# Decoder block on one core: order of split casts, small products and last outputs

## The chip, the core and the metric

The kernel runs on one core of a Trainium2 chip: TensorE (PE, with its weight loads PEld), VectorE (DVE), ScalarE (ACT), GpSimd (POOL) and SyncE (SP), each with its own instruction stream, and 16 DMA engines. The metric is device time in microseconds (us). The kernel before took 1091.79 us, the median of three runs (1090.93 to 1091.82).

## The reference

The input is x of 1024 rows by 1024 columns, all in float32. After a mixer (pooling and windowed attention, gated) comes the MLP, in which the change lies:

```python
x = x + _rmsnorm(mix, g_mix_post[l])
h2 = _rmsnorm(x, g_mlp_pre[l])
ff = jnp.einsum('bsf,fd->bsd',
                jnp.square(jax.nn.relu(jnp.einsum('bsd,df->bsf', h2, w_up[l]))), w_down[l])
x = x + _rmsnorm(ff, g_mlp_post[l])
```

w_up has 1024 by 4096 elements, w_down 4096 by 1024.

## The kernel before, in words

**Precision.** A float32 operand is split into a high part in the matmul's reduced format and a low rest: `split` (L99 to L104) is a cast on ACT (L101) and a subtraction on DVE (L104). Each product of two operands is three matmuls (`PASSES`): high x high, high x low and low x high.

**Fewer products.** Both MLP matmuls are done as a two by two block scheme with seven products instead of eight, so that sums and differences of blocks are operands too.

*Up projection* (class `Pairs`, L510 on). The 32 column blocks of w_up are taken in 16 pairs. Each pair p has seven products of 12 matmuls (4 blocks of the inner size, three passes), 128x512 each: `m1` to `m7`. `m6`, `m7` and `m4` add up in one PSUM bank ("mm", the chain): `start` (L597) copies a known part into the bank, `m6` adds and its sum is copied out (L603), `m7` adds and its sum is copied out by ACT (L612), DVE adds the bank of `m5` to that copy (L613), and `m4` adds again in the same bank, so `m4` must wait until L612 has read it. `m3` adds in the bank of `m5`. On PE the products of neighbouring pairs are interleaved: between `m7(p)` and `m4(p)` stands `m6(p+1)`. For the first pairs (p < 7) `m1` and `m2` are done ahead.

When a pair is finished, `store` (L1625 on, inside `up_close0`) forms the sums that the down projection will use as operands: additions on DVE (L1631 to L1634), for odd pairs also the small operands e (L1645 to L1648), DMAs to DRAM on SP's queue, and at its end a split of one more tile s4 (the cast on ACT reads as g<-g in the trace) and its DMA on GpSimd's queue. In iteration p of the loop the store of pair p-1 is called with m = 2(p-1), after `m3(p-1)` and before `m5(p)` and `m7(p)`. The scheduler orders what is left free; the order of the code is the priority.

*Down projection* (L1960 on). The seven products run one after the other in the order `PRODUCTS = (1, 2, 5, 3, 6, 7, 4)`, each in eight steps over the inner size: 56 steps j = 0 to 55. Products 5 and 6 (`HALVED`) are halved once more: each of their steps is seven small products (`PARTS`) of 6 matmuls of 128x256, three passes for two row tiles. The list in `quarters_mm` gives the order of the small products. Their operands are made two steps ahead (`AHEAD = 2`) in `quarters`: f2 (three blocks of e, 768 columns), w2 (four blocks of T, the sums of w, 1024 columns), w1 (three blocks of w itself, splits of 512 and 256 columns) and f1 (1024 columns). Small products 5, 6, 3 read f2 and w2, 7 and 4 read f1 and w2, 1 and 2 read f1 and w1. w1 and w2 (names ar in the trace) take buffers from a pool of six, f1 and f2 (names wh) from another of six. DVE runs in the order of the code throughout the down projection but for its last step. `SUMS` says at which step j DVE forms further sums of w in place (`first_sum` to `last_sum`, L2026 to L2038).

*The end.* In the last step of product 4 each of the row tiles n = 4 to 7 (t = 0 to 3) gets its last matmuls; DVE adds the bank (L2325), ACT squares and sums, DVE multiplies by the gain (L2123), ACT takes a square root (L130), DVE makes its inverse (L131 to L144), and `fin_out` multiplies and adds the residual in two halves (L2155) and sends them out on SP's queue. `last_tile` (L2158 on) does this for the last tile in halves.

Of the kernel before, what the change touches and what calls it, by code (L numbers as in the profile page):

```python
# [50 lines left out]
def block_kernel(ctx: ExitStack, tc, xt, x, consts, vecs, sinks, b_qkv, g_post, g_mlp, g_mlp_post,  # L51
                 w_qkv, w_u, w_g, w_pool, w_bp, w_ba, w_o, w_up, w_dn, x1_dram, spill, wbp_dram, f_dram, out):
    nc = tc.nc
# [456 lines left out]
    class Pairs:  # L510
# [98 lines left out]
        def m7(self, p, f1):  # L609
            b = self.chain[p]  # L610
            self.mm(b, p, 7, after=True)
            act.copy(f1[:, 512:], b)  # L612
            dve.tensor_tensor(f1[:, 512:], f1[:, 512:], self.fifth[p], ALU.add)  # L613
            self.f1[p] = f1

# [391 lines left out]
    def g32(shape):  # L1007
        return gp.tile([P] + shape, F32, tag="g", name=nm("g"))
# [611 lines left out]
    def up_close0(m, f):  # L1620
# [4 lines left out]
        def store():  # L1625
# [26 lines left out]
            else:  # L1652
# [2 lines left out]
                split(hi.bitcast(F32R), lo.bitcast(F32R), lo)  # L1655
                nc.gpsimd.dma_start(fd[:, 1, :], hi)
                nc.gpsimd.dma_start(fd[:, 2, :], lo)
            hi, lo = s4[:, :512], s4[:, 512:]
            split(hi.bitcast(F32R), lo.bitcast(F32R), lo)
            nc.gpsimd.dma_start(fd[:, 7:9, :], s4.rearrange("p (a b) -> p a b", b=512))  # L1660
        stores.append(store)

    stores, evens = [], []
# [236 lines left out]
    for p in range(1, NP):  # L1900
# [31 lines left out]
            up.m6(p)  # L1932
        if p > 1:
            up.m3(p - 1)
        stores.pop(0)()
        if last:
            up.rest(p, g32([S]), b6, bank("mm"), bank("at"), done=(6,))
            stores.pop(0)()
# [2 lines left out]
            up.m2(p)  # L1941
        up.m5(p, bank("at"))
        up.m7(p, g32([S]))
    flush()
    gfin_b = bcast(g_mlp_post, D)
    fpool.__exit__(None, None, None)
# [104 lines left out]
    def quarters(i, s_, ft, wt):  # L2051

        fs, w = raw_tile_of([3, 256]), halved(wt)
        nc.sync.dma_start(fs, e_dram(i, s_))
        tt = res.pop(("T", s_))
        f2, w2 = [wslot([3, 256]) for _ in range(2)], [ar([4, 256]) for _ in range(2)]
        split(*f2, fs)
        split(*w2, tt)
        w1, f1 = [ar([4, 256]) for _ in range(2)], [wslot([4, 256]) for _ in range(2)]
        for k in (slice(2, 4), slice(0, 1)):  # L2060
            split(w1[0][:, k, :], w1[1][:, k, :], w[:, k, :])
        split(*f1, halved(ft))
        opers[i, s_] = f1, f2, w1, w2

    PARTS = {1: (0, 0, 2, 0), 2: (0, 2, 2, 2), 3: (1, 2, 2, 3), 4: (0, 3, 3, 3), 5: (1, 0, 3, 0), 6: (1, 1, 3, 2),
# [7 lines left out]
    def quarters_mm(i, s_):  # L2073
        o = opers[i, s_]
        onto = ONTO if i == 6 else {}
        order = (5, 6, 3, 1, 7, 2, 4)
        if s_ == 0:
            order = (5, 6, 1, 7, 3, 2, 4) if i == 5 else (5, 6, 1, 3, 7, 2, 4)
            mine, other = ("mm", "at") if i == 5 else ("at", "mm")
            for q in order:  # L2080
                part[q] = bank(other if q in ONTO else mine, [2, 256])
                if q in onto:
                    act.copy(part[q], block_of(u4, *ONTO[q]))
        for q in order:
            fs, fk, ws, wk = PARTS[q]
            for t in range(2):
                for j, (fh, wh) in enumerate(PASSES):
                    pe.matmul(part[q][:, t, :], o[fs][fh][:, fk, t * P:(t + 1) * P], o[ws][wh][:, wk, :],  # L2088
                              start=q not in onto and (s_, t, j) == (0, 0, 0), stop=(s_, t, j) == (NS - 1, 1, 2),
                              skip_group_check=q in onto)  # L2090
# [147 lines left out]
    for s_ in range(NS):  # L2238
        SUMS[min(9 + s_, 15)].append((quarter_sums, s_))
        SUMS[(17, 18, 20, 21, 23, 24, 25, 26)[s_]].append((second_sum, s_))  # L2240
        SUMS[(25, 26, 40, 41, 22, 22, 23, 24)[s_]].append((third_sum, s_))
        SUMS[43 + s_].append((last_sum, s_))
    for s_ in range(NS):
        SUMS[27 + s_ // 2].append((quarter_sums, s_))
# [29 lines left out]
    def down_step(j, i, s_):  # L2274
# [36 lines left out]
        for t in range(4):  # L2311
# [4 lines left out]
            elif i == 4:  # L2316
# [5 lines left out]
                        last_tile(i, n, bs[t], late[-2:])  # L2322
                    continue
                down_mm(i, s_, bs, False, late)
                dve.tensor_tensor(u[t], u[t], bs[t], ALU.add)  # L2325
                fin_sq(n, 0, u[t])
                fin_gain(0, c11[t], u[t])
                rsqrt_sum(rr[:, n:n + 1], sq[:, 0, n:n + 1], sq[:, 1, n:n + 1])
                fin_out(n, (c11, v))

    with tc.manual_schedule(engines={mybir.EngineType.DVE}):
        for j in range(1, AHEAD):
# [76 lines left out]
```

## Time and profile before

| | before |
|---|---|
| median of the runs | 1091.79 us |
| profiled execution, its own time | 1090.83 us |
| its span | 1089.0 us |
| PE busy | 1077.6 us |
| DVE busy | 892.5 us |
| ACT busy | 635.9 us |

The span is what the profiler shows of the core; the profiled execution's own time holds another 1.8 us around it. In the rows of a timeline the first figure is the start in us from the span's start, the second the duration, then engine, line, operation, output<-inputs by the program's names, shape and count; in brackets stands the idle time just before and who ended it. Rows of merged instructions run from the first start to the last end; since matmuls are pipelined, the time of a group is best read from its start to the next group's start.

### The profile page before, as it was taken

The page shows a single profiled execution, that of the slowest core. Times are in us where ns is not written, and L with a number is a line of the kernel's source. Part 1 is how long each engine was busy: PE and PEld are TensorE (multiplying, and loading weights), DVE is VectorE, ACT ScalarE, POOL GpSimd, SP SyncE. Part 2 cuts the span into 40 slices and gives each one's busy share as a digit, 9 for nine tenths or more (in the row PEclk, how much of TensorE's full clock was granted, in tenths as well). Part 3 has the DMA queues.
Part 4 walks back from the last instruction along what each step waited for, and adds up shares of the span by engine and source line. Part 5 has one row for each costly group of instructions (what it writes and reads, how often), then busy time and mean ns, then how long its engine had stood idle before and what let it go on. Part 6 is the DMA issues. An engine that isn't in the chain of part 4 may idle for free.

```text
span 1089.0 us, 14897 instructions
## 1 busy us (share of the span) xinstructions
PE 1077.6 (99%) x5355; PEld 908.1 (83%) x5355; DVE 892.5 (82%) x1297; ACT 635.9 (58%) x1058; POOL 103.0 (9%) x174
## 2 busy tenths in 40 slices
PE   9999999999999999999999999999999999999996
PEld 8888888888888888888878788888888898899885
DVE  6688888999797887889987877776757889879996
ACT  7567886466654257587665555555544473275553
POOL 0354411100100012100000000001000000000000
PEclk9999999999999999999999999999999999999999
DMA  9667899689865776732567554656898687459842
GB/s 336 192 180 174 213 254 354 179 248 310 261 212 173 229 182 149 276 106 73 209 261 259 200 208 169 218 184 224 306 367 289 198 274 254 149 164 340 303 136 78
DMA packets 106618, 242.06 MB, mean 222 GB/s; under 512 B 11056, under 2 KB 28592, under 8 KB 106544
## 3 DMA queue, kind: packets, MB, share of 16 engines
q1 hardware_dynamic: 86528, 191.69, 51.8%
q0 software_dynamic: 14112, 29.37, 11.5%
q10 hardware_dynamic: 5904, 20.06, 4.7%
q8 instruction: 42, 0.69, 0.3%
q14 instruction: 32, 0.26, 0.1%
HBM read 166.63 MB, written 73.40 MB: 220 GB/s over the span
## 4 chain that ended last, share of the span: by engine, by line
PE 91%; DVE 4%; ACT 2%; DMA 2%; issue 1%; SPq 0%; DVEq 0%; ACTq 0%
PE mm L583 24%; PE at L583 16%; PE at L2114 13%; PE mm L2114 6%; PE mm L1523 5%; PE mm L2088 4%; PE at L2088 4%; PE mm L494 3%; PE sc L182 2%; PE at L1523 2%; PE at L1251 2%; PE mm L191 2%; PE mm L182 2%; PE mm L1251 1%; PE mm L496 1%; DMA g<-in_w_up_dram 1%
## 5 line engine op out<-in xcount | busy, mean ns | idle before, releaser
L2114 PE MATMUL at<-ar,wh 128*128 128x512 f32 x564 | 134.8, 389 | 0.0
L2114 PEld LDWEIGHTS at<-ar,wh 128*128 128x128 f32 x564 | 105.7, 188 | 22.3 <-DVE ar L104 0.5
L104 DVE TENSOR_TENSOR wh<-st,wh 128x512 fp32r<-128x512 f32 (+1 forms) x106 | 76.5, 731 | 29.9 <-ACT wh L101 25.5
L583 PE MATMUL mm<-T,wx 128*128 128x512 f32 x375 | 90.6, 389 | 0.0
L101 ACT CAST wh<-raw 128x1024 fp32r<-128x1024 f32 (+1 forms) x54 | 52.9, 988 | 62.9 <-PE at L2114 45.2
L583 PEld LDWEIGHTS mm<-T,wx 128*128 128x128 f32 x375 | 70.3, 188 | 14.7 <-DVE wx L104 0.2
L104 DVE TENSOR_TENSOR wh<-raw,wh 128x1024 fp32r<-128x1024 f32 (+1 forms) x54 | 61.1, 1143 | 19.9 <-ACT wh L101 19.6
L583 PE MATMUL mm<-gr,wh 128*128 128x512 f32 x321 | 77.4, 391 | 0.0
L101 ACT CAST wh<-st 128x512 fp32r<-128x512 f32 (+2 forms) x105 | 67.8, 653 | 16.0 <-PE at L583 4.9
L583 PEld LDWEIGHTS mm<-gr,wh 128*128 128x128 f32 x321 | 59.9, 188 | 12.2
L2114 PE MATMUL mm<-ar,wh 128*128 128x512 f32 x276 | 69.7, 389 | 0.0
L101 ACT CAST ar<-B 128x1024 fp32r<-128x1024 f32 (+2 forms) x59 | 42.9, 757 | 44.2 <-PE mm L2114 22.0
L583 PE MATMUL mm<-T,wh 128*128 128x512 f32 x267 | 66.3, 390 | 1.9 <-ACT g L612 1.9
L104 DVE TENSOR_TENSOR ar<-B,ar 128x1024 fp32r<-128x1024 f32 (+2 forms) x59 | 49.4, 861 | 15.0 <-ACT ar L101 15.0
L583 PEld LDWEIGHTS mm<-T,wh 128*128 128x128 f32 x267 | 50.0, 188 | 13.0 <-ACT g L612 2.7
L2114 PEld LDWEIGHTS mm<-ar,wh 128*128 128x128 f32 x276 | 51.8, 188 | 10.8
L583 PE MATMUL at<-gr,wh 128*128 128x512 f32 x243 | 59.0, 389 | 0.0
L583 PE MATMUL mm<-x,wh 128*128 128x512 f32 x240 | 58.9, 394 | 0.0
L583 PEld LDWEIGHTS at<-gr,wh 128*128 128x128 f32 x243 | 45.6, 188 | 9.5
L583 PE MATMUL at<-T,wx 128*128 128x512 f32 x213 | 52.7, 389 | 0.0
L583 PEld LDWEIGHTS mm<-x,wh 128*128 128x128 f32 x240 | 44.2, 188 | 9.6 <-ACT f L692 0.2
L583 PEld LDWEIGHTS at<-T,wx 128*128 128x128 f32 x213 | 40.0, 188 | 8.3
(556 smaller groups left out, 2466.8 us busy)
## 6 DMA issues: line engine op xcount, KB each, us to landing
raw<-f_dram SPq DMA_DIRECT2D x40, 512.0 KB, 4.4
B<-in_w_dn_dram SPq DMA_DIRECT2D x32, 512.0 KB, 6.4
st<-in_w_up_dram SPq DMA_DIRECT2D x27, 512.0 KB, 4.9
f_dram<-g SPq DMA_DIRECT2D x21, 512.0 KB, 3.2
wh<-f_dram SPq DMA_DIRECT2D x20, 512.0 KB, 5.9
g<-spill_dram SPq DMA_DIRECT2D x17, 512.0 KB, 6.0
st<-in_w_g_dram SPq DMA_DIRECT2D x16, 512.0 KB, 5.1
f_dram<-g ACTq DMA_DIRECT2D x16, 512.0 KB, 3.2
```

The lines of the kernel that those rows point to most:

```text
L101: act.copy(hi, src)
L104: return eng.tensor_tensor(lo, src, f32(hi), ALU.subtract)
L182: pe.matmul(bq, xs_[k][n // 4][:, xh, n % 4 * P:(n % 4 + 1) * P], wq[k][:, h, :], start=k == 0 and j == 0, stop=k == NK - 1 and j == 2)
L191: pe.matmul(bkv_of(n), xs_[k][n // 4][:, xh, n % 4 * P:(n % 4 + 1) * P], wkv[k // 2][:, h, k % 2, :], start=k == 0 and j == 0 and not (joi ...
L494: pe.matmul(bs[th], whi[:, k, :], rhs(k, hl, th), start=k == 0 and hl == 0, stop=False)
L496: pe.matmul(bs[th], wlo[:, k, :], rhs(k, 0, th), start=False, stop=k == nk - 1)
L583: pe.matmul(b, w[wh][:, kt, :], x_, start=not after and kt == 0 and j == 0, stop=kt == 3 and j == 2, skip_group_check=after)
L1251: pe.matmul(b, w[wh][:, kt, :], xo[xh][:, kt, :], start=not after and kt == 0 and j == 0, stop=kt == 1 and j == 2, skip_group_check=after)
L1523: pe.matmul(bs[t], Am[a][k][ah][:, t * P:(t + 1) * P], Wm[w][k][wh], start=not after and k == 0 and j == 0, stop=k == 3 and j == 2, skip_g ...
L2088: pe.matmul(part[q][:, t, :], o[fs][fh][:, fk, t * P:(t + 1) * P], o[ws][wh][:, wk, :], start=q not in onto and (s_, t, j) == (0, 0, 0), s ...
L2114: pe.matmul(bs[t], fo[fh][:, k2, t * P:(t + 1) * P], wo_[wh][:, k2, :], start=not after and s2 == 0 and k2 == 0 and j == 0, stop=(s2, k2) ...
```

## The change

Four things change, none of them in what is computed.

1. In the up projection the split at the end of `store` becomes a function of its own, `last_part`. For 0 < m < 12 the loop gets it back and issues it after `m7(p)`, with the copy L612 of that pair as the instruction behind which it may stand (`tc.issue_after`).
2. In `quarters` f1 is split ahead of w1, and in `quarters_mm` the order of the small products becomes 5, 6, 3, 7, 4, 1, 2 in all steps but the first and the last of a product.
3. `third_sum` of s_ = 2 and 3 moves from j = 40 and 41 (product 7) to j = 34 and 36 (product 6).
4. In the last step `fin_out` of tile 4 is issued behind the addition of tile 5.

```diff
         def m7(self, p, f1):
-            act.copy(f1[:, 512:], b)
+            self.copied = act.copy(f1[:, 512:], b)
...
-            hi, lo = s4[:, :512], s4[:, 512:]
-            split(hi.bitcast(F32R), lo.bitcast(F32R), lo)
-            nc.gpsimd.dma_start(fd[:, 7:9, :], s4.rearrange("p (a b) -> p a b", b=512))
+
+            def last_part():
+                hi, lo = s4[:, :512], s4[:, 512:]
+                split(hi.bitcast(F32R), lo.bitcast(F32R), lo)
+                nc.gpsimd.dma_start(fd[:, 7:9, :], s4.rearrange("p (a b) -> p a b", b=512))
+            if 0 < m < 2 * NF0 - 2:
+                return last_part
+            last_part()
...
-        stores.pop(0)()
+        part = stores.pop(0)()
...
         up.m7(p, g32([S]))
+        if part:
+            with tc.issue_after(up.copied.ins):
+                part()
...
-        w1, f1 = [ar([4, 256]) for _ in range(2)], [wslot([4, 256]) for _ in range(2)]
+        f1, w1 = [wslot([4, 256]) for _ in range(2)], [ar([4, 256]) for _ in range(2)]
+        split(*f1, halved(ft))
         for k in (slice(2, 4), slice(0, 1)):
             split(w1[0][:, k, :], w1[1][:, k, :], w[:, k, :])
-        split(*f1, halved(ft))
...
-        order = (5, 6, 3, 1, 7, 2, 4)
+        order = (5, 6, 3, 7, 4, 1, 2) if s_ < NS - 1 else (5, 6, 3, 1, 7, 2, 4)
...
-        SUMS[(25, 26, 40, 41, 22, 22, 23, 24)[s_]].append((third_sum, s_))
+        SUMS[(25, 26, 34, 36, 22, 22, 23, 24)[s_]].append((third_sum, s_))
...
-                dve.tensor_tensor(u[t], u[t], bs[t], ALU.add)
+                added = dve.tensor_tensor(u[t], u[t], bs[t], ALU.add)
+                if t == 1:
+                    with tc.issue_after(added.ins):
+                        fin_out(n - 1, (c11, v))
...
-                fin_out(n, (c11, v))
+                if t:
+                    fin_out(n, (c11, v))
```

**Where instructions stand now.** ACT in the up projection, where the store of m = 2 ends (L603 is the copy after `m6(3)`, L612 the copy after `m7(2)`, g_5194 the tile of the store's last split). Before:

```order
L597 COPY mm_5496<-f_771_4794 128x512
L101 CAST wx_5356<-ws_5353 128x512
L101 CAST g_5194<-g_5194 128x512
L603 COPY g_4671<-mm_5266 128x512
L101 CAST wx_5359<-ws_5353 128x512
L612 COPY g_5227<-mm_5147 128x512
L1683 ACTIVATE g_5227<-g_5227 128x512
```

The same place after:

```order
L597 COPY mm_5496<-f_771_4794 128x512
L101 CAST wx_5356<-ws_5353 128x512
L603 COPY g_4671<-mm_5266 128x512
L101 CAST wx_5359<-ws_5353 128x512
L612 COPY g_5224<-mm_5147 128x512
L101 CAST g_5194<-g_5194 128x512
L1688 ACTIVATE g_5224<-g_5224 128x512
```

The cast of g_5194 has moved from three places ahead of L612 to just behind it. At the end of the store of m = 10 it likewise changes places with L612, and L597 stands behind both. On PE the two filler matmuls of `m5` that stood ahead of `m4` at the stores of m = 6 and m = 10 now stand with the rest of their product; the eight at m = 2 stay.

DVE in product 5, from the operands of step 2 to those of step 3 (wh<-raw of 768 is f2, ar<-T is w2, ar<-B are the two parts of w1, wh<-raw of 1024 is f1, B<-B a `second_sum`). Before:

```order
L104 TENSOR_TENSOR wh_7839<-raw_7836,wh_7838 128x768
L104 TENSOR_TENSOR ar_7841<-T_7592,ar_7840 128x1024
L104 TENSOR_TENSOR ar_7847<-B_1122_7396,ar_7846 128x512
L104 TENSOR_TENSOR ar_7847<-B_1122_7396,ar_7846 128x256
L104 TENSOR_TENSOR wh_7849<-raw_7834,wh_7848 128x1024
L2029 TENSOR_TENSOR B_1107_7318<-B_1177_7694,B_1107_7318 128x1024
L104 TENSOR_TENSOR wh_7913<-raw_7910,wh_7912 128x768
```

The same place after:

```order
L104 TENSOR_TENSOR wh_7839<-raw_7836,wh_7838 128x768
L104 TENSOR_TENSOR ar_7841<-T_7592,ar_7840 128x1024
L104 TENSOR_TENSOR wh_7847<-raw_7834,wh_7846 128x1024
L104 TENSOR_TENSOR ar_7849<-B_1122_7396,ar_7848 128x512
L104 TENSOR_TENSOR ar_7849<-B_1122_7396,ar_7848 128x256
L2037 TENSOR_TENSOR B_1107_7318<-B_1177_7694,B_1107_7318 128x1024
L104 TENSOR_TENSOR wh_7913<-raw_7910,wh_7912 128x768
```

f1 now stands ahead of both parts of w1. On ACT the casts of a step, which the scheduler had put as w2, f2, f1, w1, now stand as f2, w2, f1, w1.

DVE at the end, from the inverse root of tile 4 (frr) to the root of tile 5 (xf_9737 is tile 4's output, at and mm the banks of the last matmuls). Before:

```order
L144 TENSOR_TENSOR frr<-sm_9799,sm_9801 128x1
L2155 SCALAR_TENSOR_TENSOR xf_9737<-v_7147,frr,xf_9737 128x512
L2155 SCALAR_TENSOR_TENSOR xf_9737<-c_1067_7148,frr,xf_9737 128x512
L2325 TENSOR_TENSOR u_7146<-u_7146,mm_9569 128x512
L2123 TENSOR_TENSOR c_1068_7149<-u_7146,bc_7131 128x512
L131 TENSOR_TENSOR sm_9825<-fsq 128x1
```

The same place after:

```order
L144 TENSOR_TENSOR frr<-sm_9799,sm_9801 128x1
L2333 TENSOR_TENSOR u_7146<-u_7146,mm_9569 128x512
L2163 SCALAR_TENSOR_TENSOR xf_9737<-v_7147,frr,xf_9737 128x512
L2163 SCALAR_TENSOR_TENSOR xf_9737<-c_1067_7148,frr,xf_9737 128x512
L2131 TENSOR_TENSOR c_1068_7149<-u_7146,bc_7131 128x512
L131 TENSOR_TENSOR sm_9825<-fsq 128x1
```

Tile 5's addition has moved ahead of tile 4's two outputs; nothing else moves at the end.

## Prediction

> **What bounds the kernel now.** First the profile's page: TensorE (PE) is busy almost throughout, so a change can only win back the few microseconds in which PE waits or is held up.
>
> ```profile
> span 1089.0 us, 14897 instructions
> PE 1077.6 (99%) x5355; PEld 908.1 (83%) x5355; DVE 892.5 (82%) x1297; ACT 635.9 (58%) x1058; POOL 103.0 (9%) x174
> ```
>
> Second, the waits of PE name one line in the up projection, L612; PE's timeline between 545 and 615 us shows both places, with the idle time and who ended it in brackets:
>
> ```profile
> 544.58 5.60 PE L583 MATMUL mm<-T,wx 128*128 128x512 f32 x24
> 550.02 1.98 PE L583 MATMUL at<-T,wx 128*128 128x512 f32 x8
> 552.98 3.03 PE L583 MATMUL mm<-T,wh 128*128 128x512 f32 x12 [0.98 <-ACT g L612]
> 555.85 2.88 PE L583 MATMUL at<-ar,wh 128*128 128x512 f32 x12
> ...
> 603.00 2.88 PE L583 MATMUL at<-gr,wh 128*128 128x512 f32 x12
> 605.72 0.61 PE L583 MATMUL at<-T,wx 128*128 128x512 f32 x2
> 607.23 3.01 PE L583 MATMUL mm<-T,wh 128*128 128x512 f32 x12 [0.90 <-ACT g L612]
> 610.08 2.88 PE L583 MATMUL mm<-T,wx 128*128 128x512 f32 x12
> ```
>
> Twice the fourth product of a pair (`m4`, mm<-T,wh) waits for the copy in `m7` (L612), which must read the bank before `m4` adds to it. Twelve matmuls of 512 columns take 2.72 us from start to start (603.00 to 605.72), 0.227 each. So the first place costs 552.98 - 550.02 - 8 x 0.227 = 1.15 us, and 0.15 more since the twelve then take 2.87: 1.30. The second costs 607.23 - 605.72 - 2 x 0.227 = 1.06 and 2.85 - 2.72 = 0.13: 1.19.
>
> Third, ScalarE's (ACT) timeline says why the copy was late:
>
> ```profile
> 550.66 0.62 ACT L101 CAST g<-g 128x512 fp32r<-128x512 f32 x1 [1.91 <-DVE g L1634]
> 551.19 0.58 ACT L603 COPY g<-mm 128x512 f32<-128x512 f32 x1
> 551.67 0.62 ACT L101 CAST wx<-ws 128x512 fp32r<-128x512 f32 x1
> 552.34 0.59 ACT L612 COPY g<-mm 128x512 f32<-128x512 f32 x1
> ...
> 603.06 0.62 ACT L101 CAST wh<-st 128x512 fp32r<-128x512 f32 x1 [0.40 <-DVE st L539]
> 606.08 0.62 ACT L101 CAST g<-g 128x512 fp32r<-128x512 f32 x1 [2.39 <-DVE g L1634]
> 606.60 0.58 ACT L612 COPY g<-mm 128x512 f32<-128x512 f32 x1
> ```
>
> Both times ACT stands before the cast of `store`'s last part (g<-g), which waits for VectorE (DVE, L1634), with the copy queued behind it.
>
> Fourth, the stretch of down's first halved product (product 5, L2088), by the groups of its window and PE's timeline:
>
> ```profile
> L2088 PE MATMUL mm<-ar,wh 128*128 128x256 f32 x192 | 26.5, 285 | 0.0
> L2088 PE MATMUL at<-ar,wh 128*128 128x256 f32 x144 | 19.9, 283 | 0.0
> ```
>
> ```profile
> 868.03 3.04 PE L2088 MATMUL mm<-ar,wh 128*128 128x256 f32 x24
> ...
> 876.82 1.60 PE L2088 MATMUL at<-ar,wh 128*128 128x256 f32 x12
> 878.26 1.60 PE L2088 MATMUL mm<-ar,wh 128*128 128x256 f32 x12
> ...
> 898.69 1.79 PE L2088 MATMUL mm<-ar,wh 128*128 128x256 f32 x12
> ...
> 903.92 1.90 PE L2088 MATMUL mm<-ar,wh 128*128 128x256 f32 x12
> ...
> 909.25 0.86 PE L2114 MATMUL at<-ar,c12f 128*128 128x512 f32 x3
> ```
>
> Twelve of these take 1.44 us from start to start (876.82 to 878.26), so 192 + 144 = 336 need 40.32. The stretch takes 909.25 - 868.03 = 41.22: 0.90 us is lost in slivers of 0.1 to 0.3, seen in twelves of 1.79 and 1.90 where others have 1.60. The second halved product, product 6, has the same 336 matmuls and loses nothing:
>
> ```profile
> 952.84 2.31 PE L2088 MATMUL at<-ar,wh 128*128 128x256 f32 x18
> ...
> 993.16 0.86 PE L2114 MATMUL mm<-ar,hold 128*128 128x512 f32 x3
> ```
>
> It takes 993.16 - 952.84 = 40.32.
>
> The busy time of PE hardly shows those slivers. In the view by windows, with the columns window, length, then PE, PEld, DVE, ACT, POOL:
>
> ```profile
> 900.00:925.00 25.00, 24.96 (x146) 21.93 (x146) 24.93 (x27) 9.00 (x11) 0.00 (x0) 1.00 0.74 253
> ```
>
> By PE's busy column this window loses 0.04 us, though one of the slivers above lies in it; I take the starts, 0.90. The Trainium skill (Perfetto Trace Analysis, Identifying the Most-Contended Engine) says that matmul busy time is a poor measure of TensorE's distance from its limit, since matmuls are pipelined. The trace agrees, 0.04 against 0.90; by busy time the sum below would be 2.4 instead of 3.2.
>
> **The change part by part.**
>
> *Up, one split behind the copy.* Work is the same; the cast, its subtraction and its GpSimd DMA are moved behind L612 in five pairs (m = 2 to 10), and both stalls lie in them (the store chains at m = 2 and 10). First place: the copy now stands behind L603 and one cast only. L603 reads what the 24 matmuls leave at 544.58 + 5.60 = 550.18. From L603's start to L612's end it was 552.93 - 551.19 = 1.74, so the copy ends at about 551.95 and `m4` starts at about 552.0 instead of 552.98: 0.97 won of 1.30; the rest stays, since PE would be ready at 551.84. Second place: the copy follows the cast of 603.06 and ends by about 604.3. PE, 0.97 earlier and without the two filler matmuls ahead (they run later), wants it at 605.72 - 0.97 = 604.75. All 1.19 is won. Next late there: L597 (the bank that the next pair's `m6` adds to) stands behind the moved cast, which cannot start before 606.08 if DVE's chain stays where it is. One cast (0.52, as 606.08 to 606.60) and one copy (0.58) later it is done at 607.2, while PE wants it at 604.75 + 2.72 = 607.5. The cover is 0.3 us. The moved cast comes at about 551.95 instead of 550.66 in the first place; behind it hang its subtraction, which DVE now has after L613 instead of ahead of it, and a DMA on GpSimd's queue, where nothing else waits in this stretch. Nothing of it feeds PE in the up projection; it can only hold its buffer, and with it a later load of w_up, about 1 us longer: 0, and up to 1 against us. Sum of this part 2.16, bounds 0 (the second stall turns into a wait for L597, and a load comes 1 us late) and 2.49.
>
> *Down, order of splits and small products.* The same five casts, five subtractions and 42 matmuls per step, in another order. DVE and ACT in product 5:
>
> ```profile
> 878.27 1.03 DVE L104 TENSOR_TENSOR ar<-B,ar 128x512 fp32r<-128x512 f32 x2 [0.80 <-ACT ar L101]
> 879.21 1.22 DVE L104 TENSOR_TENSOR wh<-raw,wh 128x1024 fp32r<-128x1024 f32 x1
> 880.35 1.22 DVE L2029 TENSOR_TENSOR B<-B,B 128x1024 f32<-128x1024 f32 x1
> 881.48 0.95 DVE L104 TENSOR_TENSOR wh<-raw,wh 128x768 fp32r<-128x768 f32 x1
> 882.35 1.22 DVE L104 TENSOR_TENSOR ar<-T,ar 128x1024 fp32r<-128x1024 f32 x1
> ...
> 902.95 1.23 DVE L104 TENSOR_TENSOR ar<-T,ar 128x1024 fp32r<-128x1024 f32 x1
> ```
>
> ```profile
> 877.62 0.93 ACT L101 CAST ar<-B 128x512 fp32r<-128x512 f32 x2 [1.26 <-PE at L2088]
> ```
>
> The slivers at the starts of steps follow DVE: ar<-T (w2) ends at 902.95 + 1.14 = 904.09, in the middle of the slow twelve from 903.92. DVE is late because it stood 0.80 us before w1 (ar<-B x2), whose cast waits until PE has let go of a buffer late in the step before, with f1 (wh<-raw of 1024) ready behind it. Now f1 stands ahead and fills that wait, and PE asks for w1 at the sixth small product instead of the fourth (2 x 0.72 us later), having let go of w2 after the fifth instead of the seventh. With 0.80 us less waiting, w2 at 903.9 would be there 0.8 earlier, against slivers of at most 0.30. I take the whole 0.90; bounds 0 (DVE is full anyway: 24.93 of 25 in the window above) and 0.90, and a loss only by the third rival below. Product 6 gets the same order where nothing is to be won: 0. The last step keeps the old order.
>
> *The sums moved to j = 34 and 36:* two DVE instructions leave the start of product 7, where PE waits for nothing, and come into product 6. The first of them:
>
> ```profile
> 997.87 1.23 DVE L2029 TENSOR_TENSOR B<-B,B 128x1024 f32<-128x1024 f32 x1
> ```
>
> A step there lasts 5.04 us (7 x 0.72), and DVE's five subtractions take 0.87 + 1.14 + 1.14 + 0.94 = 4.09, so one of 1.14 fills a step (5.23) with 0.2 over, paid from the lead of the others: 0. Without that cover it would cost 2 x 0.2 = 0.4.
>
> *The end.* DVE runs one loop per tile:
>
> ```profile
> 1073.30 0.68 DVE L2325 TENSOR_TENSOR u<-u,mm 128x512 f32<-128x512 f32 x1
> ...
> 1075.09 0.16 DVE L136 RECIPROCAL sm<-sm 128x1 f32<-128x1 f32 x1 [0.17 <-ACT sm L130]
> ...
> 1077.26 0.68 DVE L2325 TENSOR_TENSOR u<-u,mm 128x512 f32<-128x512 f32 x1
> ```
>
> This loop is 3.96 us and holds one wait of 0.17 for ACT's square root. With tile 4's two outputs behind tile 5's addition, ACT's square and root run beside them, and that one wait goes: 0.17; bounds 0 (the addition now waits for PE) and 0.2. Tile 4's DMAs leave one addition later, with three tiles' DMAs behind them: 0.
>
> Sum: 0.97 + 1.19 + 0.90 + 0.17 = 3.23 us. The profiled execution took 1090.83 (span 1089.0 and 1.8 around it) and would take 1087.6. It lies 0.96 under the median of the runs, 1091.79; taken from that: 1088.6.
>
> **The rivals.**
>
> *One part fails.* Either DVE stays the bound in product 5 (for: 24.93 of 25, and 4.09 + 1.14 = 5.23 us of work in a step of 5.04 that has a sum; against: the wait of 0.80, which a full engine would not have), or in the up projection PE, earlier by 2 us, meets the next late thing, L597 or the weights behind a load of w_up. The price is 0.9 or 1.2: 1089.5 or 1089.8, right at the limit of 0.2% (2.2 us, at 1089.6), which is about what a measurement of this kernel can tell from no change.
>
> *Hardly anything is left.* Both fail: 1091.79 - 0.97 - 0.17 = 1090.7, or 1091.6 if the first stall turns into another wait as well, for instance because the store chain that feeds it hangs on a load of w_up and not on PE.
>
> *Slower: the loads of e gate w2.* ACT's order now has f2's cast ahead of that of T (w2); before, T was first and f2 waited for its load behind it:
>
> ```profile
> 900.77 1.79 ACT L101 CAST wh<-raw 128x768 fp32r<-128x768 f32 x2 [0.84 <-DMA raw<-spill_dram]
> ```
>
> That load landed 900.77 - 898.69 = 2.1 us into its step. Two casts, of 768 and 1024, take 1.8 (this row's x2) and the subtraction of w2 1.2, which puts w2 at 5.1, just at the end of the step of 5.04. If loads land 2.5 in, each of some 13 steps of both products loses 0.45: 5.9 lost instead of 0.9, less 2.3 from the rest: 1091.79 + 5.0 - 2.3 = 1094.5. It decides from 2.0 us on. Against it: a load's buffer comes free with the subtraction of f1, which moves ahead by w1's 0.94 and the wait of 0.80, so the landing should move to about the step's start.
>
> **How the numbers follow.** Forecast 0.62 (1088.6; from 1090.83 less all upper bounds, 3.59, = 1087.2 up to 1089.6); one part fails 0.20; hardly anything left 0.11; slower 0.07. Of the second case a fifth lies under 1089.6, so faster is 0.66, same 0.27, slower 0.07. The range 1087.2 to 1090.9 leaves out the slower case, half of hardly anything, and a little at the low end, 0.15 in all.
>
> **What would show it.** In the profile after: no wait of PE for L612, or one under 0.2 us near 552; the stretch of product 5 at 40.3 to 40.5 us from start to start; DVE's waits before ar<-B there gone; product 6 still 40.3; the loops of the end 3.96 but for one of 3.8. The prediction is wrong if PE waits for L597 or wx near 606, if product 5 still takes 41.2, or if casts of 768 wait for the spill load while PE is held at the start of steps.

## The result, and the profile after

The changed kernel takes 1088.92 us (median of 8 runs, 1088.54 to 1089.13), the kernel before, run beside it, 1091.94 (8 runs, 1090.93 to 1093.12). The ratio of the medians is 0.9971, with a 95% interval from 0.9960 to 0.9982: faster by 3.0 us, or 0.29%, with the whole interval under 1. The forecast was 1088.6. Its total is right; its terms are less so, as the two traces show.

Inserted lines move the numbers: L2088 is now L2096, L2114 is L2122, L2325 is L2333, L2155 is L2163. The head of the page, then the longest of PE's waits over the whole span of the changed kernel (us in total, times, longest):

```profile
span 1087.3 us, 14910 instructions
PE 1077.3 (99%) x5355; PEld 908.3 (84%) x5355; DVE 892.2 (82%) x1297; ACT 635.9 (58%) x1058; POOL 101.6 (9%) x174
```

```profile
PE mm L583 <- ACT g L612: 0.9, 1, 0.9
```

PE's busy time fell by 0.3 us between the two profiles where the span fell by 1.7; most of what is won was idle time. One wait for L612 is left. PE's timeline in the up projection tells which:

```profile
545.41 5.60 PE L583 MATMUL mm<-T,wx 128*128 128x512 f32 x24
550.85 1.98 PE L583 MATMUL at<-T,wx 128*128 128x512 f32 x8
553.77 3.01 PE L583 MATMUL mm<-T,wh 128*128 128x512 f32 x12 [0.94 <-ACT g L612]
...
603.76 2.88 PE L583 MATMUL at<-gr,wh 128*128 128x512 f32 x12
606.49 2.88 PE L583 MATMUL mm<-T,wh 128*128 128x512 f32 x12
609.21 2.88 PE L583 MATMUL mm<-T,wx 128*128 128x512 f32 x12
```

The second stall (607.23 before) is gone: three twelves follow each other at 2.72 to 2.73 us. The first is still there: 553.77 - 550.85 - 8 x 0.227 = 1.11, and 0.13 more in the twelve behind it (3.01 long where others have 2.88), 1.24 where it was 1.30; the experiments show that this 0.06 is scatter. ACT's timeline at both places:

```profile
551.53 0.62 ACT L101 CAST wx<-ws 128x512 fp32r<-128x512 f32 x1
553.13 0.58 ACT L612 COPY g<-mm 128x512 f32<-128x512 f32 x1 [0.97 <-DVE g L1646]
553.61 0.62 ACT L101 CAST g<-g 128x512 fp32r<-128x512 f32 x1
...
603.97 0.59 ACT L612 COPY g<-mm 128x512 f32<-128x512 f32 x1
605.70 0.62 ACT L101 CAST g<-g 128x512 fp32r<-128x512 f32 x1 [1.14 <-DVE g L1634]
606.68 0.57 ACT L597 COPY mm<-at 128x512 f32<-128x512 f32 x1 [0.37 <-PE at L583]
```

The cast does stand behind the copy now, both times. But the first copy has a wait of its own, for a line that the prediction never named: L1646, an instruction of the store for the operand e. DVE's timeline has it:

```profile
552.68 0.42 DVE L1646 TENSOR_TENSOR g<-g,g 128x256 f32<-128x256 f32 x1
```

It ends at 553.10 and the copy starts at 553.13. At the second place L597, feared as the next late thing, is done at 606.68 + 0.57 = 607.25, and PE adds to its bank at 609.21: not late.

Down: PE's timeline through products 5 and 6.

```profile
867.60 3.04 PE L2096 MATMUL mm<-ar,wh 128*128 128x256 f32 x24
...
874.08 1.02 PE L2096 MATMUL at<-ar,wh 128*128 128x256 f32 x6
...
908.06 0.86 PE L2122 MATMUL at<-ar,c12f 128*128 128x512 f32 x3
...
951.60 2.31 PE L2096 MATMUL at<-ar,wh 128*128 128x256 f32 x18
...
991.92 0.86 PE L2122 MATMUL mm<-ar,hold 128*128 128x512 f32 x3
```

Product 5 takes 908.06 - 867.60 = 40.46 instead of 41.22, product 6 still 40.32. One sliver of 0.14 is left, in the six of 1.02 us (others take 0.88). DVE and then ACT a little behind it:

```profile
876.44 1.21 DVE L104 TENSOR_TENSOR wh<-raw,wh 128x1024 fp32r<-128x1024 f32 x1
877.58 1.02 DVE L104 TENSOR_TENSOR ar<-B,ar 128x512 fp32r<-128x512 f32 x2
```

```profile
871.28 1.05 ACT L101 CAST wh<-raw 128x1024 fp32r<-128x1024 f32 x1 [1.04 <-PE at L2096]
...
876.46 0.93 ACT L101 CAST ar<-B 128x512 fp32r<-128x512 f32 x2 [0.39 <-PE at L2096]
877.90 0.84 ACT L101 CAST wh<-raw 128x768 fp32r<-128x768 f32 x1 [0.51 <-PE at L2096]
```

DVE does f1 (1024 columns) while ACT still waits before w1, and has no wait of its own before w1. ACT's cast of f2 (768 columns) waits for PE, not for the load of e.

The end, on DVE: the loop over tiles, from tile 4's addition to tile 7's.

```profile
1068.02 0.69 DVE L2333 TENSOR_TENSOR u<-u,at 128x512 f32<-128x512 f32 x1 [3.17 <-PE at L2122]
...
1070.74 0.69 DVE L2333 TENSOR_TENSOR u<-u,mm 128x512 f32<-128x512 f32 x1
1071.35 0.74 DVE L2163 SCALAR_TENSOR_TENSOR xf<-v,frr,xf 128x512 f32<-128x512 f32 x1
...
1072.67 0.68 DVE L2131 TENSOR_TENSOR c<-u,bc 128x512 f32<-128x512 f32 x1
1073.28 0.15 DVE L131 TENSOR_TENSOR sm<-fsq 128x1 f32<-128x1 f32 x1
1073.35 0.15 DVE L136 RECIPROCAL sm<-sm 128x1 f32<-128x1 f32 x1
...
1079.47 0.68 DVE L2181 TENSOR_TENSOR u<-u,mm 128x512 f32<-128x512 f32 x1
```

1079.47 - 1068.02 = 11.45. Before, the same stretch:

```profile
1069.26 0.69 DVE L2325 TENSOR_TENSOR u<-u,at 128x512 f32<-128x512 f32 x1 [3.16 <-PE at L2114]
...
1074.01 0.69 DVE L2123 TENSOR_TENSOR c<-u,bc 128x512 f32<-128x512 f32 x1
1074.77 0.16 DVE L131 TENSOR_TENSOR sm<-fsq 128x1 f32<-128x1 f32 x1
...
1081.22 0.68 DVE L2173 TENSOR_TENSOR u<-u,mm 128x512 f32<-128x512 f32 x1
```

1081.22 - 1069.26 = 11.96, so 0.51 is won.

By the two traces the parts give 0.06 + 1.19 + 0.76 + 0.51 = 2.52 us. The profiled executions themselves differ by only 1090.83 - 1089.07 = 1.76, since the one of the changed kernel lost 0.8 to 0.9 in its first matmuls, which the change doesn't touch: the first twelve (L182) last 4.09 us instead of 3.21, and the next group, L191, starts at 8.68 instead of 7.79.

That start is different in every execution: the first L191 began at 7.73 in the quickest of the fourteen profiles of this study (e12) and at 10.68 in the slowest (e11). It is part of the runs' scatter. The medians differ by 3.0, half a microsecond more than the parts, and the kernel before scatters over 2.2 us. Nothing here shows where that half belongs. Two stretches in which profiles that keep the old code there differ among themselves are the second stall, where PE waits 0.90 us before, 2.28 in e2, 2.11 in e3 and 0.70 in e4, and product 6, which takes 40.31 to 40.32 in all profiles but e4's, and 40.87 there.

### The profile page after: what moved, and what is told of

Same layout as the page of the kernel before. It is cut to its first block, busy times and chain, and to the rows that moved or that the text cites. A ratio compares the mean times of both kernels' runs of the same rounds, so it can differ in the third digit from the quotient of the medians.

```text
span 1087.3 us, 14910 instructions
## 1 busy us (share of the span) xinstructions
PE 1077.3 (99%) x5355; PEld 908.3 (84%) x5355; DVE 892.2 (82%) x1297; ACT 635.9 (58%) x1058; POOL 101.6 (9%) x174
## 4 chain that ended last, share of the span: by engine, by line
PE 93%; DVE 3%; DMA 1%; ACT 1%; issue 1%; DVEq 0%; SPq 0%; ACTq 0%
PE mm L583 25%; PE at L583 17%; PE at L2122 13%; PE mm L2122 6%; PE mm L1523 5%; PE at L2096 4%; PE mm L2096 4%; PE mm L494 3%; PE sc L182 2%; PE at L1523 2%; PE at L1251 2%; PE mm L191 2%; PE mm L182 2%; PE mm L1251 2%; PE mm L496 1%; PE sc L456 1%
## 5 line engine op out<-in xcount | busy, mean ns | idle before, releaser
L2122 PE MATMUL at<-ar,wh 128*128 128x512 f32 x564 | 134.6, 389 | 0.0
L2122 PEld LDWEIGHTS at<-ar,wh 128*128 128x128 f32 x564 | 105.8, 188 | 22.2 <-DVE ar L104 0.3
L2122 PE MATMUL mm<-ar,wh 128*128 128x512 f32 x276 | 69.5, 389 | 0.0
L2122 PEld LDWEIGHTS mm<-ar,wh 128*128 128x128 f32 x276 | 51.8, 188 | 10.8
L2096 PE MATMUL at<-ar,wh 128*128 128x256 f32 x336 | 47.5, 283 | 0.0
```

The source lines that it names most:

```text
L2122: pe.matmul(bs[t], fo[fh][:, k2, t * P:(t + 1) * P], wo_[wh][:, k2, :], start=not after and s2 == 0 and k2 == 0 and j == 0, stop=(s2, k2) ...
```

## The experiments

Each kernel was timed beside the kernel before; the ratios are to it, with their 95% intervals. e1 to e4 ran together on one chip, so did e5 to e8 at another time, and so did e9 to e12; only kernels that ran together are compared. The changed kernel took 1088.92 us in the result above and 1088.38 as e9, so half a microsecond between these groups means nothing.

**e1: the up part alone**, on the kernel before: the copy kept as `self.copied`, and

```
+        if part:
+            with tc.issue_after(up.copied.ins):
+                part()
```

> The kernel before with the up projection's part of the change alone. Theory (the first stall is the copy L612 waiting for its output buffer, which the last small operand e of the store still reads, the second is the queue on ACT): the wait at m = 2 stays at 0.9 to 1.0 us, the one at m = 10 is gone, and the stretch from the 24 matmuls before the first stall to the end of the up projection is 1.2 us shorter than before; time 1.2 us under before. Rival (both stalls are the ACT queue, and the profile after was an odd execution): both waits gone, 2.2 us under before. Product 5 keeps its 41.2 us and the end its 11.96 us from the addition of tile 4 to that of tile 7.

Measured: 1090.37 us against 1091.98, ratio 0.9986 (0.9977 to 0.9995). In PE's timeline the second stall is gone, and the first is left:

```profile
553.13 3.03 PE L583 MATMUL mm<-T,wh 128*128 128x512 f32 x12 [0.89 <-ACT g L612]
```

The wait is as long as in the whole change. So the other parts have no hand in it.

**e2: f1's split ahead of w1 alone**, with the old order of small products and the old places of the sums.

```
-        w1, f1 = [ar([4, 256]) for _ in range(2)], [wslot([4, 256]) for _ in range(2)]
+        f1, w1 = [wslot([4, 256]) for _ in range(2)], [ar([4, 256]) for _ in range(2)]
+        split(*f1, halved(ft))
...
-        split(*f1, halved(ft))
```

> The kernel before with f1 split ahead of w1 in both halved products, small products in the old order. Theory (the waits of DVE before w1 are what makes w2 late): DVE's waits before ar<-B shrink, product 5 takes 40.4 to 40.7 us from start to start instead of 41.2; time 0.5 to 0.8 us under before. Rival (PE has to ask for w1 later, too): w1, now behind f1, comes late for the fourth small product, and product 5 takes 41.2 us or more, product 6 more than 40.3.

Measured: 1091.30 against 1091.98, ratio 0.9993 (0.9985 to 1.0002), which by itself is no difference. PE's timeline, with the starts of product 5, of what follows it and of product 7, and a wait near the end of product 4, the last product:

```profile
871.82 3.04 PE L2088 MATMUL mm<-ar,wh 128*128 128x256 f32 x24
...
912.27 0.86 PE L2114 MATMUL at<-ar,c12f 128*128 128x512 f32 x3
...
996.13 0.86 PE L2114 MATMUL mm<-ar,hold 128*128 128x512 f32 x3
...
1067.49 0.73 PE L2114 MATMUL at<-ar,wh 128*128 128x512 f32 x2 [0.45 <-DVE ar L104]
```

Product 5 takes 40.45: this one line carries the whole gain there. But from the start of product 7 to tile 4's addition, which DVE starts at 1072.81 (all of product 7 and most of product 4), it is 1072.81 - 996.13 = 76.68, where it was 1069.26 - 993.16 = 76.10 before and is 1068.02 - 991.92 = 76.10 after the whole change. Of 0.77 won, 0.58 is given back later, in product 4; e5 shows how.

**e3: the order of small products alone**, with w1's split still ahead of f1's.

```
-        order = (5, 6, 3, 1, 7, 2, 4)
+        order = (5, 6, 3, 7, 4, 1, 2) if s_ < NS - 1 else (5, 6, 3, 1, 7, 2, 4)
```

> The kernel before with the new order of the small products alone, w1 still split ahead of f1. Theory (DVE order decides, but w1's buffers come free 0.7 us earlier in this order): DVE's wait before ar<-B falls from 0.80 to under 0.2 us, product 5 takes 40.5 to 40.8 us. Rival (f1, asked for at the fourth small product and still split last, is now the late one): product 5 at 41.2 us or more with slow groups in the middle of steps. Time 0 to 0.7 us under before.

Measured: 1092.21 against 1091.98, ratio 1.0009 (1.0000 to 1.0017), slower by 0.2 us if at all. The same wait in PE's timeline:

```profile
1067.73 1.43 PE L2114 MATMUL at<-ar,wh 128*128 128x512 f32 x5 [0.63 <-DVE ar L104]
```

Product 5 takes 912.11 - 870.73 = 41.38; with the old splits and the old order it takes 41.22 before, 41.21 in e1 and 41.59 in e4. Alone the new order wins nothing, and products 7 and 4 lose more than in e2: by the starts of the same two instructions, 996.19 and 1073.08, they take 76.89. PE was not ahead here, so the loss does not come of PE's being early.

**e4: the end alone**, `fin_out(n - 1, ...)` behind the addition of t = 1.

> The kernel before with the change at the end alone. Theory (the gain there is 0.5 us, since steps of DVE that hang on the one before start 0.1 to 0.15 us later than steps that do not, besides the wait of 0.17): from the addition of tile 4 to that of tile 7 11.45 us instead of 11.96. Rival (only the wait of 0.17 goes, the rest in the profile after came from elsewhere): 11.8. Product 5 and the stalls of the up projection as before. Time 0.2 to 0.5 us under before.

Measured: 1091.26 against 1091.98, ratio 0.9995 (0.9986 to 1.0004), which by itself is no difference. The trace is sharper: DVE's first and last addition,

```profile
1070.22 0.69 DVE L2325 TENSOR_TENSOR u<-u,at 128x512 f32<-128x512 f32 x1 [3.18 <-PE at L2114]
...
1081.67 0.68 DVE L2173 TENSOR_TENSOR u<-u,mm 128x512 f32<-128x512 f32 x1
```

stand 11.45 apart, as in the whole change. The 0.51 is the end's own.

**e5: the whole change, but the sums back** at j = 40 and 41.

```
-        SUMS[(25, 26, 34, 36, 22, 22, 23, 24)[s_]].append((third_sum, s_))
+        SUMS[(25, 26, 40, 41, 22, 22, 23, 24)[s_]].append((third_sum, s_))
```

> The changed kernel with the two third sums back at j = 40 and 41. Theory (the move costs and brings nothing): product 6 at 40.3 us, the first steps of product 7 without waits of PE, time as the changed kernel within 0.3 us. Rival (the move keeps PE from a wait at the start of product 7 now that PE comes earlier): a wait of PE of some tenths in product 7, time 0.3 to 1 us above the changed kernel.

Measured: 1088.40, ratio 0.9963 (0.9950 to 0.9975); e6, which turned out to run like the changed kernel, took 1088.32 beside it. By the medians nothing; by the trace something. From the start of product 7 to tile 4's addition it takes 1067.57 - 991.17 = 76.40 instead of 76.10, and the 0.30 is lost before one group in product 4. PE, then DVE, of e5:

```profile
1060.78 1.29 PE L2122 MATMUL mm<-ar,wh 128*128 128x512 f32 x5
1062.23 1.43 PE L2122 MATMUL at<-ar,wh 128*128 128x512 f32 x5
```

```profile
1060.95 1.22 DVE L104 TENSOR_TENSOR ar<-B,ar 128x1024 fp32r<-128x1024 f32 x1
```

DVE's last split of w ends at 1060.95 + 1.22 = 1062.17 and the group of 1062.23 starts behind it; five matmuls take 1.14, so PE would have been there at 1061.92. The same place of the kernel before, DVE, then PE:

```profile
1062.67 1.22 DVE L104 TENSOR_TENSOR ar<-B,ar 128x1024 fp32r<-128x1024 f32 x1
```

```profile
1062.77 1.29 PE L2114 MATMUL mm<-ar,wh 128*128 128x512 f32 x5
```

There the split ends at 1062.67 + 1.22 = 1063.89 and PE would be ready at 1062.77 + 1.14 = 1063.91 (its next group starts at 1063.95): just in time, with no lead. After the whole change it is just in time again (split done at 1062.65, PE ready at 1062.67).

The two sums of w themselves stand more than 60 us ahead of this place, at the start of product 7. What makes DVE late is a wait some 17 us ahead of it, in product 4, where DVE's first multiplication by the gain needs ACT's square and sum. Before, then e5:

```profile
1045.07 0.69 DVE L2123 TENSOR_TENSOR v<-v,bc 128x512 f32<-128x512 f32 x1 [0.92 <-ACT junk L2120]
```

```profile
1043.57 0.69 DVE L2131 TENSOR_TENSOR v<-v,bc 128x512 f32<-128x512 f32 x1 [1.11 <-ACT junk L2128]
```

Counted from the start of product 7 the gain stands at 1045.07 - 993.16 = 51.91 before and at 1043.57 - 991.17 = 52.40 in e5, and from there to its last split of w DVE hardly waits in either. ACT's order in the traces differs: before, and after the whole change, it makes two split casts and then that square; in e5 it makes three. From the start of the first of these casts to the gain it is 2.65 before and 3.60 in e5, 0.95 more, which is one cast from start to start. e2 and e3 have the third cast there too (their gains stand at 52.72 and 52.90), and of the fourteen profiles just these three do, and just these three lose in this stretch: 0.58, 0.79 and 0.30, where the others take 76.10 to 76.13. So each of these three edits lets the scheduler put ACT's casts in another order; this is read from the rows, and no run moves that cast alone.

**e6: the copy's tile asked for earlier.** In pair 2, f1 is taken from its pool before the store takes its tiles.

```
+        f1 = g32([S]) if p == 2 else None
         part = stores.pop(0)()
...
-        up.m7(p, g32([S]))
+        up.m7(p, f1 or g32([S]))
```

> The changed kernel with the output tile of the copy at m = 2 (f1 of pair 2) taken from its pool ahead of the store's tiles, so that it doesn't get the buffer that the store's last e still reads. Theory (the buffer is the cause of the first stall): the wait of PE for L612 near 553 us falls from 0.94 to under 0.2 us, L612 starts about 0.5 us after the cast before it, time 0.8 to 1.2 us under the changed kernel, if no store tile that now gets that buffer makes DVE late. Rival (L603 and the cast ahead of the copy are the cause): the wait stays at 0.9.

Measured: 1088.32 (1087.86 to 1088.40), and PE waits 0.97 for L612 as ever. The edit did not do what it was for. The addresses that the built programs give to four tiles of the pool (bytes in a partition, read from the programs and not from the trace) tell why:

```
tile                                          after     e6        e10
older even tile of e, last read by L1646      140512    140512    140512
f1 of pair 1, last read in L1634              111840    111840    111840
s4 of pair 2's store                          107744    107744    140512
f1 of pair 2, the copy's output               140512    140512    111840
```

The kernel before, e1 and e7 have the four addresses of the first column, too. With either text the copy's output gets the buffer of the even tile that the store's last L1646 reads. The copy must wait for that read.

**e7: that read made earlier by one instruction**: both L1646 ahead of both L1647 (the third instruction for each e).

```
-                for i, a, b in ((5, t0[:, 0, :], t[:, 0, :]), (6, t0[:, 1, :], s2)):
-                    e = g32([3, 256])
+                pieces = ((5, t0[:, 0, :], t[:, 0, :], g32([3, 256])), (6, t0[:, 1, :], s2, g32([3, 256])))
+                for i, a, b, e in pieces:
                     dve.tensor_tensor(e[:, 1, :], b[:, 256:], a[:, 256:], ALU.subtract)
                     dve.tensor_tensor(e[:, 0, :], e[:, 1, :], a[:, :256], ALU.add)
+                for i, a, b, e in pieces:
                     dve.tensor_tensor(e[:, 2, :], b[:, :256], e[:, 1, :], ALU.subtract)
```

> The changed kernel with the four instructions of the store that read the older tile (L1645, L1646 of both e) ahead of the two that don't (L1647). The older tile's buffer comes free one instruction of 0.33 us earlier. Theory (the buffer is the cause): the first stall falls by about 0.33 us, from 0.94 to 0.6. Rival (ACT's queue): 0.94 stays.

Measured: 1087.92 (1087.85 to 1088.31), ratio 0.9960 (0.9948 to 0.9972). DVE's and ACT's rows:

```profile
551.53 0.76 DVE L1646 TENSOR_TENSOR g<-g,g 128x256 f32<-128x256 f32 x2
```

```profile
552.32 0.59 ACT L612 COPY g<-mm 128x512 f32<-128x512 f32 x1 [0.55 <-DVE g L1646]
```

The read ends at 552.29, the copy starts at 552.32, and its wait is 0.55 instead of 0.97. From the store's first addition on DVE (L1631) to the copy's start it is 4.47, where it is 4.80 to 4.81 in the other kernels with the whole change and the store's old order: 0.33 less, one instruction. The copy follows the read. PE's wait falls from 0.97 (e6) to 0.52, more than the 0.33 that the edit accounts for; that wait scatters from run to run (0.69 in e9, which is the changed kernel). The median is 0.40 under e6's, with runs that overlap.

**e8: tile 5's outputs, too, behind tile 6's addition.**

```
-                if t == 1:
+                if t:
                     with tc.issue_after(added.ins):
                         fin_out(n - 1, (c11, v))
...
-                if t:
+                if t == 2:
                     fin_out(n, (c11, v))
```

> The changed kernel with tile 5's outputs, too, behind the addition of tile 6. Theory (each turn saves the hanging steps and the wait, 0.5 us, as long as PE has the tile ready): from the addition of tile 4 to that of tile 7 10.9 to 11.1 us instead of 11.45; time 0.4 us under the changed kernel. Rival (tile 6's last matmuls end too late, at about the time at which DVE has the root of tile 5): at most 0.1 us won.

Measured: 1087.94 (1087.89 to 1088.15), ratio 0.9960 (0.9947 to 0.9972). DVE's addition of tile 6:

```profile
1073.79 0.69 DVE L2333 TENSOR_TENSOR u<-u,mm 128x512 f32<-128x512 f32 x1 [0.46 <-PE mm L2122]
```

From tile 4's addition to tile 7's it is 1078.55 - 1067.22 = 11.33, 0.12 less than with one tile moved: now tile 6's addition comes too early for PE, and waits 0.46. The bound has passed to PE. The median is 0.38 under e6's, of which the trace accounts for 0.12.

**e9: the changed kernel again**, beside the last three.

> The changed kernel itself, as the yardstick for the three kernels beside it. Expected: 1088.3 to 1088.9 us; PE waits 0.9 to 1.0 us for L612 near 553, product 5 takes 40.46, the end from tile 4's addition to tile 7's 11.45.

Measured: 1088.38 (1087.79 to 1088.68), ratio 0.9971 (0.9960 to 0.9983). Product 5 takes 40.45, the end 11.46; PE's wait for L612 is 0.69, and the first place loses 0.97 in all, 0.27 less than in the first profile: the store's chain on DVE starts a little earlier against PE there.

**e10: the even tile's last read 1.2 us earlier.** In the store of m = 2 the two instructions in front of the six for e (the difference in f, L1633, and the write of s4, L1634) go behind them.

```
+            def fourth():
+                dve.tensor_tensor(f[:, 512:], f[:, :512], f[:, 512:], ALU.subtract)
+                dve.tensor_tensor(s4[:, 512:], g[:, :512], t[:, 1, :], ALU.subtract)
+            if m != 2:
+                fourth()
...
+            if m == 2:
+                fourth()
             q.dma_start(fd[:, 5:7, :], t)
```

> The changed kernel, with two DVE instructions of the second store (the difference in f and the one in s4) behind the six for the operand e. Theory (the copy L612 waits until the last read of the older even tile gives its buffer free): that read ends at about 551.9 instead of 553.1, before ACT is through with the cast ahead of the copy (552.05), so the copy starts at about 552.05 and PE, ready at 552.67, never waits: the first place loses 0.1 instead of 1.24, and the kernel is 1.1 to 1.2 us faster than the changed kernel beside it. Rival (ACT's queue or the store's whole chain holds the copy): the copy still starts near 553.1 and the time is the same within 0.3. A second rival: the next late thing there (the addition L613, or the cast that now waits for the later s4) takes the place; then only 0.3 to 0.8 is won.

Measured: 1088.78 (1088.46 to 1089.38), ratio 0.9970 (0.9961 to 0.9979): 0.40 slower than e9, where 1.1 faster was expected. DVE (L1636 is the write of s4), and ACT:

```profile
552.79 0.68 DVE L1636 TENSOR_TENSOR g<-g,g 128x512 f32<-128x512 f32 x1
```

```profile
553.50 0.59 ACT L612 COPY g<-mm 128x512 f32<-128x512 f32 x1 [1.36 <-DVE g L1636]
```

The even tile is free at 551.92 (its last read starts at 551.51 and takes 0.41), as expected, but the copy no longer gets its buffer. With the store's instructions in another order the pool deals its buffers out anew (the table above): s4 takes the even tile's, and the copy's output that of the f1 of pair 1, whose last read is L1636. It ends at 553.47, and the copy starts at 553.50. The expected gain fell with that; the cause stands firmer, since the copy now waits for exactly the instruction that frees its new buffer. From the store's first addition to the copy's start it is 5.13 instead of 4.80, so 0.33 of the loss is the edit's; PE loses 1.40 at the place instead of e9's 0.97.

**e11: e10 with e8's end.**

> As the kernel before it, and at the end tile 5's outputs too stand behind tile 6's addition. Expected from the run that did this alone (11.33 instead of 11.45 from tile 4's addition to tile 7's): 0.1 to 0.4 us under the kernel before it, 1.2 to 1.6 under the changed kernel. If it is slower than that kernel, the end loses at the last tile what it wins at tile 6.

Measured: 1088.72 (1087.87 to 1091.02), ratio 0.9972 (0.9963 to 0.9981). The end takes 1081.41 - 1070.08 = 11.33 as in e8. By the median, 0.06 under e10 is nothing, and it isn't faster than e9: the 1.2 to 1.6 that was expected did not come, since e10's buffer is part of it.

**e12: e11 with the old order of the small products** in the middle steps (5, 6, 3, 1, 7, 2, 4).

> As the kernel before it, but the small products of the middle steps in the order of the kernel before the change (5, 6, 3, 1, 7, 2, 4), f1's split still first. Theory (the split ahead of w1 does it all): product 5 takes 40.45 as with the new order, and the time is that of the kernel before it within 0.2. Rival (asking for w1 later and letting go of w2 earlier has a share): product 5 loses 0.2 to 0.8 more.

Measured: 1088.91 (1087.48 to 1090.41), ratio 0.9974 (0.9964 to 0.9984), 0.2 above e11, whose runs overlap its own. Product 5 takes 908.11 - 867.65 = 40.46, as with the new order, and from product 7's start to tile 4's addition it is 76.11. The new order of the small products does nothing, alone (e3) or in company.

A kernel that joins e7 and e8 was not run, and no version is shown to beat the changed kernel by more than the scatter; e7, 0.40 under e6 by the medians and 0.33 by the trace, is the nearest to it.

## Why the prediction was right, point by point

**The first stall: wrong, 0.97 forecast and nothing won that stands clear of scatter.** The step that failed is "the copy now stands behind L603 and one cast only". It took the queue on ACT for the only reason why the copy was late. There were two, and the other one already ended last. Before the change, ACT's queue was free for the copy at about 551.67 + 0.52 = 552.19 (0.52 as from 606.08 to 606.60); the second L1646, which frees the buffer of the copy's output, ended at 551.89 + 0.42 = 552.31, as DVE's timeline of the kernel before has it:

```profile
551.89 0.42 DVE L1646 TENSOR_TENSOR g<-g,g 128x256 f32<-128x256 f32 x1
```

The copy started at 552.34. In every profile it starts 0.02 to 0.04 after the end of the instruction that frees that buffer. The 0.15 between the two causes is not printed at the copy's row, so the timeline showed only the queue. From the store's first addition on DVE (L1631) to the copy's start it is 4.79 to 4.81 in the kernel before, e1 to e4, the changed kernel, e5, e6, e8 and e9, whether the cast is moved or not; 4.47 in e7; and 5.13 to 5.15 in e10, e11 and e12. So moving the cast left the copy where it was, and the 0.06 between the two traces is scatter: PE's wait here is 0.57 to 0.98 in the four profiles with the old order (before, e2, e3, e4) and 0.69 to 1.01 in the six with the cast moved and the old store. e7 and e10 move the copy both ways by moving the instruction that frees its buffer: that cause is shown. That the whole loss goes with it isn't: the copy never got a buffer that was free early.

**The second stall: right.** 1.19 forecast and won, with the reason given. At m = 10 the output's buffer is not in the way (the copy of 603.97 has no wait of its own), and L597 was done at 607.25, as forecast (607.2); PE wanted it at 609.21, since it was not ahead by the 0.97 of the first place, and so the cover was wider than the 0.3 forecast. None of the ten profiles with the cast moved has a wait there. How much it is worth differs with the run, by the 0.70 to 2.28 that PE waits with the old order.

**Product 5: right in cause, 0.90 forecast, 0.76 won.** DVE's wait before w1 is gone because f1 fills it (e2: the split alone gives 40.45). The second reason given, that PE asks for w1 two small products later, has no share (e3, e12), and the kernel says why: in the list `PARTS`, small product 3 reads f2 and w1, not f2 and w2. So PE asks for w1 at the third small product in both orders.

The 0.14 left lie in step 1, at just that third small product (874.08). The second of its matmuls, the first that reads the low part of w1, starts at 874.24; DVE's split of w1 ended at 874.18. That split stood behind f1's (872.36), whose cast on ACT started at 871.28 after 1.04 us of waiting for PE. This chain is read from the rows; no run changes it.

The prediction's 0.04 of busy time against 0.90 by the starts compares two stretches: the window is 25 us long, the product 41. In that window the slow twelve loses 905.65 - 903.92 - 1.44 = 0.29, still far more than the 0.04.

**The sums: 0, right by the sum and incomplete in its reason.** They were taken for harmless where they stood, in a product in which PE waits for nothing. Left there with the rest of the change, they cost 0.30 (e5), and the split or the new order alone costs 0.58 or 0.79 (e2, e3), though not in product 7: ACT's casts come in another order in product 4, where DVE was just in time. The step missed asking what a move does to the order of the other engines later on.

**The end: right in kind, 0.17 forecast, 0.51 won.** The mis-sized term is "holds one wait of 0.17". ACT's timeline before, at tile 5:

```profile
1074.55 0.19 ACT L2120 ACTIVATION_READ_ACCUMULATOR junk<-u 128x1 f32 x1
1074.77 0.29 ACT L130 ACTIVATE sm<-fsq 128x1 f32<-128x1 f32 x1
```

DVE's L131 started at 1074.77, at the end of ACT's sum, and its reciprocal at 1075.09, at the end of ACT's root: two waits, not one. From the gain (L2123, 1074.01) to the reciprocal it was 1.08. With the two outputs between the addition and the gain, ACT is through by then, and it is 1073.35 - 1072.67 = 0.68. That is 0.40. The other 0.10 is the addition and what follows it: 0.71 from start to start where the next instruction reads the sum (1073.30 to 1074.01), 0.61 where it doesn't (1070.74 to 1071.35). The first of the two waits has no bracket in DVE's timeline; the start-to-start distances hold it.

**The rivals.** "One part fails" is what happened in the up projection, in the first place instead of the second, and by a wait that was not on the list. "The loads of e gate w2" did not come: f2's casts wait for PE. That the total came out near 3 us is partly luck: the errors of the terms (-0.91, -0.14, +0.34 by the two traces) partly cancel, and the median moved half a microsecond more than the traces' parts. The fit of the total is no proof of the terms.

## What to carry to other kernels

An instruction that stands behind a waiting one in a queue may have a second wait that ends a little later, and where the time between the two is short the profile shows only the queue. Before costing a move past the queue, look at what else the instruction needs, and above all at whose buffer its output takes: the last reader of that buffer is a wait like any other, and any reordering may deal the buffers out anew (e10).

A reordering can also change the order in which another engine works much later. In e2, e3 and e5 ACT made one cast more ahead of a square that DVE needed, and 0.3 to 0.8 us were lost at a place where DVE had been just in time. So after each change compare the same stretches to the end of the kernel, and not only the stretch that the change was for.

## What was not expected of the hardware

In these traces two steps of 512 columns on DVE start 0.60 to 0.61 us apart where the second doesn't read the first's result (1070.74 to 1071.35), though each is shown as 0.68 to 0.74 long, and 0.71 apart where it does (1073.30 to 1074.01); for steps of one column it is 0.07 (1073.28 to 1073.35) where they don't depend on each other. So at the end of this kernel the order alone was worth 0.1 us for one such pair.

The first matmuls of the program end at another time in each execution: the group behind them starts at 7.73 to 10.68 us over fourteen profiles. In the slowest (e11) PE stood 1.29 there for ACT, and ACT had stood 1.54 for a load of x. The spread is as much as the whole change wins, and reason enough to compare stretches and not spans.
